# All low parts of the sample's output weights on VectorE, and small buffers given out by how long they have been free

## The chip, the cores and the metric

The kernel runs on one core of a Trainium2 chip. The metric is the device time of one execution in microseconds (us). Before the change it was 1543.17 us, the median of three runs (1542.73, 1543.17 and 1548.15).

## The reference

The kernel computes one layer of an encoder for two inputs that share all weights: a *prompt* of 512 tokens and a *sample* of 1024 tokens, each with 1024 features. Cut to what matters:

```python
h = _rmsnorm(x, norm_attn_g);  z = h @ w_in          # 1024 -> q 512, k 128, v 128, ca 512, cb 512
a_out = _window_attn(q, k, v, bias, band, sink)      # 8 heads, 2 kv heads, |q - k| <= 128
c = _dwconv(ca * sigmoid(cb), conv_dw_w, conv_dw_b)  # 31 taps
c = silu(_layernorm(c, conv_ln_g, conv_ln_b))
x = x + concat([a_out, c]) @ w_out
h = _rmsnorm(x, norm_ffn_g)
u = _dwconv(h @ w_up, ffn_dw_w, ffn_dw_b)            # 3 taps, 2 x 2816 columns
x = x + (silu(u[:, :2816]) * u[:, 2816:]) @ w_down
y = _rmsnorm(x, norm_final_g)
```

Everything is float32. To keep its precision on TensorE, each operand is split into a high part (rounded to the engine's reduced format) and a low part (the rest), and each product is three matmuls: high x high, low x high, high x low.

## The kernel before

**Stages.** The program is written as a main stream of TensorE work with a *side* generator that feeds other work between its pieces. In order:

1. The prompt's `w_in` projection.
2. The sample's `w_in` projection: 14 chunks of 128 columns of `w_in` by two halves of 512 tokens. Its side is `prompt()`: the attention of the prompt (units 0 to 7), the normalisation of its conv branch (`conv_norm`), and the prompt's `w_out` product (`out_half`). The 31 taps of the convolutions are offered to VectorE, ScalarE and GpSimd all the while.
3. The prompt's up projection with its gate (`ffn_step`, 22 steps). Its side is `sample()`: the attention of the sample (units 8 to 23), and then loads and splits of the sample's `w_out` and half of its conv normalisation.
4. The sample's `w_out` product, its up and down projections (with sums and differences of halves that save products; TensorE's order there is written out by hand), and the final norms.

**Who sets the order.** A list scheduler decides, when the program is built, in which order each engine gets its instructions, up to stage 4's hand-written part; it follows the dependences among instructions, and the buffers are among them. Each engine then takes its instructions strictly in that order, so an instruction that waits holds up all that stand behind it on that engine. Another buffer for a tile means another dependence, and so another order on every engine.

**Buffers.** `Slots` hands out SBUF buffers by size: 2 KB buffers (names `h...`), 4 KB ones (`q...`, 15 of them) and two more kinds (`c`, `d`). A request of at most 2 KB (one 128x512 float32 tile) takes the first free buffer of the smallest size that fits; only when none under 4 KB is free is a `q` buffer cut into two halves, as long as more than `KEEP` = 3 of them are free. "First" means the one that has stood longest in the list of free buffers; but a tile can be "free" in this sense while transfers or instructions on it are still to run, and the next owner waits for them.

**Weights.** A chunk is loaded from HBM as raw float32, then `split` makes the high part (`L202`, a cast on ScalarE) and the low part (`L203`, a subtraction raw - high, on GpSimd, or on VectorE if `dve` is set). For `w_in` and `w_up` a chunk is 128x1024 and all low parts are on GpSimd. For the sample's `w_out` there are 16 chunks of 128x512, split in `sample()` by

```python
split_wo((m - WOA) // 2, m % 2, m % 4 < DW2)     # DW2 = 0: none on VectorE
```

**Names and lines.** Products of `w_in` and `w_up` are `L309`, `L310` and `L312` (tiles `b` and `u` in PSUM, two banks each). `b` is emptied by ScalarE `L385`, `L398` and VectorE `L394`, `L399`, `L409`; the rows of q go to HBM by `L403` (`qsd`). Attention: scores `L585`, `L592`, `L603` to `L620`; transposes `L641`, splits `L643`, `L644`, values `L655`, `L656`; rows to HBM `L671` (`catd`). Taps: `L353`, `L356` on ScalarE, `L357` on GpSimd, `L364`, `L372` on VectorE. `conv_norm`: transposes of the conv rows `L700` (PE), statistics `L702`, `L703` (VectorE), reciprocal root `L186`, `L187` (GpSimd), scaling `L706` (VectorE), transposes back `L712` (PE), swish `L715` to `L720`. `w_out`: loads `L761`, `L763`, products `L736` to `L738`. Up projection's gate: `u` is read by ScalarE `L866` and twice by VectorE `L862`; `L886`, `L888`, `L889`, `L891`, `L892` make the gate, `L893` stores it.

Of the kernel before, what the change touches and what calls it, by code (L numbers as in the profile page):

```python
# [15 lines left out]
P = 128  # L16
# [31 lines left out]
SCB, SCD = "aapa", "aaap"  # L48


WOP, WOA, DW, DW2 = 1, 5, 2, 0
NE = 2
YN = 2
OB = "uc"
# [4 lines left out]

BACK = (200, 1500)  # L60
U0 = 2


FILL = 216
# [2 lines left out]
class Slots:  # L67
# [3 lines left out]


    def __init__(self, pool, classes, halved=None, keep=0):
        self.pool, self.free, self.n = pool, [], 0
        self.halved, self.keep, self.halves = halved, keep, {F32: [], F32R: []}
        for kind, (count, size) in classes.items():
            for i in range(count):
                self.free.append((f"{kind}{i}", size))

    def tile(self, shape, dt=F32, nbytes=4, among=None):  # L80
        need = nbytes
        for s in shape:
            need *= s
        fits = [s for s in self.free if s[1] >= need and (among is None or s[0][0] in among)]
        if self.halved and nbytes == 4 and need <= 2048 and not any(s[1] < 4096 for s in fits):
            halves = self.halves[dt]
            if not halves and sum(s[0][0] == self.halved for s in fits) > self.keep:
                slot = next(s for s in fits if s[0][0] == self.halved)
                self.free.remove(slot)
                self.n += 1  # L90
                whole = Whole(self, slot, dt, (self.pool(slot[0]) if callable(self.pool) else self.pool).tile([P, 2, 512], dt, tag=slot[0], name=f"{slot[0]}_{self.n}", bufs=1))
                halves += [(whole, 0), (whole, 1)]
                whole = None
            if halves:
                return Half(*halves.pop(0), shape)
        if not fits:
            raise RuntimeError(f"no slot for {need} bytes")
        least = min(s[1] for s in fits)
        slot = next(s for s in fits if s[1] == least)
        self.free.remove(slot)  # L100
        self.n += 1
        return Held(self, slot, (self.pool(slot[0]) if callable(self.pool) else self.pool).tile([P] + list(shape), dt, tag=slot[0], name=f"{slot[0]}_{self.n}", bufs=1))


class Held:
# [4 lines left out]
        return self.t[i]  # L110

    def __del__(self):
        self.slots.free.append(self.slot)


class Whole:
# [6 lines left out]
class Half:  # L123
# [14 lines left out]
    def __del__(self):  # L138
        w = self.whole
        w.out -= 1  # L140
        if w.out:
            w.slots.halves[w.dt].append((w, self.i))
        else:
            w.slots.halves[w.dt] = [h for h in w.slots.halves[w.dt] if h[0] is not w]
            w.slots.free.append(w.slot)


@with_exitstack
def tile_hybrid_encoder(ctx: ExitStack, tc: tile.TileContext, xs, rel_bias, norm_attn_g, w_in,
# [17 lines left out]
    sb = Slots(lambda tag: homes[tag[0]], dict(q=(15, 4096), c=(4, 4224), h=(61, 2048), d=(2, 2176), s=(32, 64)), "q", KEEP)  # L167
# [133 lines left out]
    def drain(queue):  # L301
        while queue:
            advance(queue)
# [422 lines left out]
    def out_half(i, n):  # L726
        G, b = blocks[i]
        if i not in xr:
            xr[i] = load_x(G, b)
        x = xr[i]  # L730
        po = bank("out")
        s = slice(n * NT, (n + 1) * NT)
        for kc in range(KC):
            wh, wl = wo[kc, n]
            ch, cl = (t[:, kc % 4, :] for t in cats[i, kc // 4])
            nc.tensor.matmul(po[:], ch, wh[:], start=(kc == 0), stop=False)  # L736
            nc.tensor.matmul(po[:], ch, wl[:], start=False, stop=False)  # L737
            nc.tensor.matmul(po[:], cl, wh[:], start=False, stop=(kc == KC - 1))  # L738
            if kc % 2 == 1 and kc < KC - 1:
                yield 0.0  # L740
        nc.vector.tensor_tensor(x[:, s], po[:], x[:, s], op=ALU.add)
        if n == 1:
            x1[i] = x
            nc.sync.dma_start(x1d[i][:], x[:])
            ss = sm(1)
            junk = sb.tile([D], BF16, 2)
            nc.scalar.activation(junk[:], x[:], AF.Square, accum_out=ss[:])
            rstd_of(ss[:], D, rs2[:, i:i + 1])
            cats.pop((i, 0)), cats.pop((i, 1))
            xr.pop(i)  # L750
        yield 0.0
# [83 lines left out]
    drain(side)  # L835
    load_kv()
    drain(convs)


    def want_up(k, half):  # L840
# [103 lines left out]
    for k in range(NJ):  # L944
        if k == U0:
            side.append(sample())
# [418 lines left out]
    need = {1: B11, 2: B21, 5: B12, 6: B22, 4: B21, 3: B22}  # L1365
# [305 lines left out]
```

## Time and profile before

| | us |
|---|---|
| median of three runs | 1543.17 |
| the profiled execution, its own time | 1547.91 |
| its span in the profile | 1546.1 |
| TensorE busy | 1491.7 (96%) |
| VectorE busy | 1125.0 (73%) |
| ScalarE busy | 795.3 (51%) |
| GpSimd busy | 704.0 (46%) |

The profiled execution is 4.7 us over the median of the runs shown. TensorE has 54.4 us in which no matmul runs. Stage 2 lies at about 109 to 318 us of the span, stage 3 at about 350 to 670, the sample's `w_out` product behind it to about 790. In the profile, "PE" is TensorE, "DVE" VectorE, "ACT" ScalarE, "POOL" GpSimd, "SP" the queue that issues the transfers; the column PEclk is the mean clock granted to TensorE, 1.00 being full speed.

### The profile page before, as it was taken

The page shows a single profiled execution, that of the slowest core. Times are in us where ns is not written, and L with a number is a line of the kernel's source. Part 1 is how long each engine was busy: PE and PEld are TensorE (multiplying, and loading weights), DVE is VectorE, ACT ScalarE, POOL GpSimd, SP SyncE. Part 2 cuts the span into 40 slices and gives each one's busy share as a digit, 9 for nine tenths or more (in the row PEclk, how much of TensorE's full clock was granted, in tenths as well). Part 3 has the DMA queues.
Part 4 walks back from the last instruction along what each step waited for, and adds up shares of the span by engine and source line. Part 5 has one row for each costly group of instructions (what it writes and reads, how often), then busy time and mean ns, then how long its engine had stood idle before and what let it go on. Part 6 is the DMA issues. An engine that isn't in the chain of part 4 may idle for free.

```text
span 1546.1 us, 20081 instructions
## 1 busy us (share of the span) xinstructions
PE 1491.7 (96%) x6843; PEld 1228.5 (79%) x6843; DVE 1125.0 (73%) x1608; ACT 795.3 (51%) x1404; POOL 704.0 (46%) x562
## 2 busy tenths in 40 slices
PE   8999998899999999899999999999999899999998
PEld 6787787787888888777777888888888788888886
DVE  7998767857879795434677777777776855668885
ACT  4644654335777776713454544555445633343355
POOL 7652343225667766956423555555545000003345
PEclk9999999899999999999999999999999999999999
DMA  6572334447344435868422233333331582356654
GB/s 226 163 216 80 104 102 125 130 132 223 103 130 130 131 121 165 257 215 287 158 82 69 96 107 105 102 103 102 103 133 51 194 299 86 108 166 214 211 184 163
DMA packets 228780, 227.17 MB, mean 147 GB/s; under 512 B 13268, under 2 KB 168348, under 8 KB 228549
## 3 DMA queue, kind: packets, MB, share of 16 engines
q1 hardware_dynamic: 228677, 225.88, 45.4%
q8 instruction: 54, 0.88, 0.2%
q14 instruction: 49, 0.40, 0.1%
HBM read 164.74 MB, written 62.14 MB: 147 GB/s over the span
## 4 chain that ended last, share of the span: by engine, by line
PE 72%; DMA 4%; DVE 2%; POOL 2%; ACT 2%; issue 1%; SPq 1%; POOLq 0%; ACTq 0%; DVEq 0%
PE w L1091 8%; PE w L1090 8%; PE w L1089 8%; PE w L1423 7%; PE w L1424 7%; PE w L1425 7%; PE u L312 5%; PE u L309 5%; PE u L310 5%; PE u L736 1%; PE u L738 1%; PE u L737 1%; DMA h<-gt 1%; PE b L309 1%; PE b L310 1%
## 5 line engine op out<-in xcount | busy, mean ns | idle before, releaser
L203 POOL TENSOR_TENSOR q<-q,q 128x1024 fp32r<-128x1024 f32 x72 | 173.5, 2415 | 93.6 <-ACT q L202 37.6
L965 POOL TENSOR_TENSOR q<-q,q 128x512 fp32r<-128x512 f32 x101 | 140.7, 1399 | 157.9 <-ACT q L1075 145.8
L965 DVE TENSOR_TENSOR h<-h,h 128x512 fp32r<-128x512 f32 (+2 forms) x202 | 158.2, 816 | 63.1 <-ACT h L969 24.3
L1423 PE MATMUL w<-h,h 128*128 128x512 f32 x462 | 179.8, 389 | 0.6 <-ACT h L969 0.6
L1425 PE MATMUL w<-h,h 128*128 128x512 f32 x462 | 179.8, 389 | 0.0
L1424 PE MATMUL w<-h,h 128*128 128x512 f32 x462 | 179.7, 389 | 0.0
L1089 PE MATMUL w<-h,q 128*128 128x512 f32 x448 | 175.1, 391 | 3.9 <-ACT w L1181 2.2
L1091 PE MATMUL w<-h,q 128*128 128x512 f32 x448 | 174.5, 389 | 1.1 <-POOL q L965 1.1
L309 PE MATMUL u<-h,q 128*128 128x512 f32 x400 | 160.0, 400 | 7.7 <-DVE h L862 4.6
L1090 PE MATMUL w<-h,q 128*128 128x512 f32 x426 | 165.8, 389 | 0.0
L310 PE MATMUL u<-h,q 128*128 128x512 f32 x400 | 157.9, 395 | 0.0
L312 PE MATMUL u<-h,q 128*128 128x512 f32 x384 | 152.4, 397 | 1.3 <-POOL q L203 1.3
L364 DVE SCALAR_TENSOR_TENSOR c<-c,cvw,c 128x512 f32<-128x512 f32 x184 | 138.0, 750 | 2.9
L962 POOL TENSOR_TENSOR q<-q,q 128x1024 f32<-128x1024 f32 x12 | 32.8, 2742 | 235.6 <-DMA h<-gb 195.5
L969 ACT CAST h<-h 128x512 fp32r<-128x512 f32 x120 | 71.7, 620 | 96.7 <-DVE h L965 47.7
L309 PE MATMUL b<-h,q 128*128 128x512 f32 x256 | 102.8, 401 | 4.0 <-DVE d L394 2.9
L1089 PEld LDWEIGHTS w<-h,q 128*128 128x128 f32 x448 | 84.1, 188 | 22.5 <-ACT w L1181 2.6
L862 DVE SCALAR_TENSOR_TENSOR h<-u,fw,h 128x511 f32<-128x511 f32 x88 | 65.4, 743 | 50.3 <-ACT h L866 49.5
L1423 PEld LDWEIGHTS w<-h,h 128*128 128x128 f32 x462 | 86.7, 188 | 19.1 <-ACT h L969 1.0
L310 PE MATMUL b<-h,q 128*128 128x512 f32 x256 | 101.5, 396 | 0.0
L312 PE MATMUL b<-h,q 128*128 128x512 f32 x256 | 101.5, 396 | 0.0
L1425 PEld LDWEIGHTS w<-h,h 128*128 128x128 f32 x462 | 86.7, 188 | 18.1
(417 smaller groups left out, 3656.1 us busy)
## 6 DMA issues: line engine op xcount, KB each, us to landing
q<-in_w_up SPq DMA_DIRECT2D x88, 512.0 KB
ga<-q SPq DMA_DIRECT2D x64, 256.0 KB
h<-ga SPq DMA_DIRECT2D x57, 256.0 KB
q<-in_w_in SPq DMA_DIRECT2D x28, 512.0 KB
h<-in_w_down SPq DMA_DIRECT2D x52, 256.0 KB
q<-in_x_sample SPq DMA_DIRECT2D x15, 512.0 KB
h<-qsd SPq DMA_DIRECT2D x24, 256.0 KB
x1d<-q SPq DMA_DIRECT2D x11, 512.0 KB
```

Source lines behind the costliest of these rows:

```text
L203: (nc.vector if dve else nc.gpsimd).tensor_tensor(lo[:], raw[:], hi[:].bitcast(F32), op=ALU.subtract)
L309: nc.tensor.matmul(out, whi[:, kc, :], hi[:], start=(kc == 0), stop=False)
L310: nc.tensor.matmul(out, whi[:, kc, :], lo[:], start=False, stop=False)
L312: nc.tensor.matmul(out, wlo[:, kc, :], hi[:], start=False, stop=(kc == KC - 1))
L364: nc.vector.scalar_tensor_tensor(acc[:], src(t), w(t), acc[:], op0=ALU.mult, op1=ALU.add)
L965: (eng or nc.vector).tensor_tensor(out, a, b, op=ALU.subtract)
L1089: nc.tensor.matmul(out, whi[:, s], hi[:], start=(start and c == 0), stop=False, **go)
L1090: nc.tensor.matmul(out, whi[:, s], lo[:], start=False, stop=False, **go)
L1091: nc.tensor.matmul(out, wlo[:, s], hi[:], start=False, stop=(stop and c == 3), **go)
L1423: nc.tensor.matmul(out, sh[:, c], th[:], start=(p == 0), stop=False)
L1424: nc.tensor.matmul(out, sh[:, c], tl[:], start=False, stop=False)
L1425: nc.tensor.matmul(out, sl[:, c], th[:], start=False, stop=(p == NPAIR - 1))
```

## The change

Two parts.

1. `DW2` goes from 0 to 4: the low parts of all 16 chunks of the sample's `w_out` are made on VectorE.
2. `Slots` counts its requests (`clock`) and notes at which count each buffer or half buffer came free. A request of at most 2 KB now takes the one of (first free small buffer, oldest free half) that has been free longer. While `sb.old` is 24 (stage 2 from the point at which its side is added, until its rest is drained; 0 elsewhere), a `q` buffer may also be cut in two when the small buffer came free fewer than 24 requests ago and the first free `q` buffer has been free for longer than it; 3 free `q` buffers are still kept whole.

```diff
-WOP, WOA, DW, DW2 = 1, 5, 2, 0
+WOP, WOA, DW, DW2 = 1, 5, 2, 4
...
+OLD = 24
...
+    def give(self, slot):
+        self.since[slot[0]] = self.clock
+        self.free.append(slot)
+
+    def split_whole(self, slot, dt):
...
+        since = self.since.get(slot[0], -OLD)
+        self.halves[dt] += [(whole, 0, since), (whole, 1, since)]
+
     def tile(self, shape, dt=F32, nbytes=4, among=None):
+        self.clock += 1
...
-        if self.halved and nbytes == 4 and need <= 2048 and not any(s[1] < 4096 for s in fits):
+        least = min((s[1] for s in fits), default=0)
+        slot = next((s for s in fits if s[1] == least), None)
+        if self.halved and nbytes == 4 and need <= 2048:
             halves = self.halves[dt]
...
+            wholes = [s for s in fits if s[0][0] == self.halved]
+            since = self.since.get(slot[0], -OLD) if slot and slot[1] < 4096 else self.clock
+            if halves and (min(h[2] for h in halves) < since or since == self.clock):
+                return Half(*self.oldest(halves), shape)
+            if (since == self.clock or self.clock - since < self.old) and len(wholes) > self.keep and \
+                    self.since.get(wholes[0][0], -OLD) < since:
+                self.split_whole(wholes[0], dt)
+                return Half(*self.oldest(halves), shape)
...
     side.append(prompt())
+    sb.old = OLD
...
     drain(convs)
+    sb.old = 0
```

What the change does to the instructions shows at three places. In the listings each row is a line of code, an operation, its output and inputs and its shape; numbers behind a name count buffers and tiles. In the changed kernel the lines of the code have moved by 20 (`L309` to `L329`, `L700` to `L720`, `L712` to `L732`, `L202` to `L222`, `L203` to `L223`) or 22 (`L862` to `L884`, `L866` to `L888`).

The first place is TensorE at the end of the conv normalisation of the prompt, near the end of stage 2. Before:

```order
L310 MATMUL b_149_2657<-h_106_666,q_382_2515 128x512
L312 MATMUL b_149_2657<-h_105_665,q_383_2516 128x512
L700 MATMUL a_142_2526<-ident,q_370_2402 128x128 x4
L712 MATMUL u_144_2556<-ident,q_387_2538 128x128 x4
L700 MATMUL a_150_2684<-ident,h_400_2676 128x128 x4
L712 MATMUL u_152_2717<-ident,h_404_2696 128x128 x4
L655 MATMUL a_148_2618<-h_391_2600,h_162_970 128x512
L736 MATMUL u_154_2828<-h_418_2781,h_216_1325 128x512
```

And now, at the last of the four conv blocks:

```order
L330 MATMUL b_151_2694<-h_150_884,q_364_2497 128x512
L720 MATMUL a_150_2669<-ident,h_385_2661 128x128 x4
L332 MATMUL b_151_2694<-h_149_883,q_365_2498 128x512
L329 MATMUL b_153_2791<-h_83_541,q_380_2637 128x512
L330 MATMUL b_153_2791<-h_84_542,q_380_2637 128x512
L332 MATMUL b_153_2791<-h_83_541,q_381_2638 128x512
L329 MATMUL b_153_2791<-h_85_557,q_380_2637 128x512
L330 MATMUL b_153_2791<-h_86_558,q_380_2637 128x512
L332 MATMUL b_153_2791<-h_85_557,q_381_2638 128x512
L756 MATMUL u_154_2809<-q_247_1580,q_205_1264 128x512
```

Before, the two transposes there and the two back of the last two blocks stood one behind the other with no projection between. Now 34 matmuls of 128x512 (projection and `w_out`) stand between the last block's transposes and its transposes back, and many more between those of the block before; and some tiles of 2 KB are named `q` now (`q_247`, `q_205`).

The second place is ScalarE near the end of stage 3, where it empties the products `u` and casts the high parts of `w_out`. Before:

```order
L866 ACTIVATE h_1003_6447<-u_362_6380,vecs,fw 128x512
L202 CAST h_1052_6643<-h_1031_6549 128x512
L202 CAST h_1035_6563<-h_1014_6490 128x512
L886 ACTIVATE b_364_6522<-h_1003_6447 128x512
L202 CAST h_1012_6480<-h_990_6399 128x512
L866 ACTIVATE h_1022_6512<-u_363_6455,vecs,fw 128x512
L202 CAST h_1015_6492<-h_997_6428 128x512
```

And now:

```order
L222 CAST h_1022_6572<-h_1008_6517 128x512
L888 ACTIVATE h_983_6427<-u_362_6360,vecs,fw 128x512
L908 ACTIVATE b_364_6502<-h_983_6427 128x512
L888 ACTIVATE h_1002_6492<-u_363_6435,vecs,fw 128x512
L222 CAST h_995_6472<-h_977_6408 128x512
L222 CAST h_1015_6543<-h_994_6470 128x512
L222 CAST h_1024_6588<-h_999_6486 128x512
```

The three casts that stood between the emptying of `u_362` and that of `u_363` are gone from there.

The third place is VectorE in the same stretch. Before:

```order
L862 SCALAR_TENSOR_TENSOR h_980_6362<-u_358_6315,fw,h_980_6362 128x511 x2
L665 TENSOR_TENSOR h_979_6349<-b_360_6331,h_957_6218 64x512
L862 SCALAR_TENSOR_TENSOR h_1003_6447<-u_362_6380,fw,h_1003_6447 128x511 x2
L888 SCALAR_TENSOR_TENSOR b_364_6522<-b_364_6522,h_1003_6447 128x512
L862 SCALAR_TENSOR_TENSOR h_1022_6512<-u_363_6455,fw,h_1022_6512 128x511 x2
```

And now:

```order
L884 SCALAR_TENSOR_TENSOR h_960_6342<-u_358_6295,fw,h_960_6342 128x511 x2
L223 TENSOR_TENSOR h_1010_6520<-h_986_6442,h_1009_6519 128x512
L223 TENSOR_TENSOR h_979_6412<-h_969_6376,h_978_6411 128x512
L223 TENSOR_TENSOR h_1018_6554<-h_991_6458,h_1017_6553 128x512
L223 TENSOR_TENSOR h_988_6445<-h_971_6382,h_987_6444 128x512
L223 TENSOR_TENSOR h_1033_6624<-h_1011_6529,h_1032_6623 128x512
L685 TENSOR_TENSOR h_959_6329<-b_360_6311,h_937_6198 64x512
L223 TENSOR_TENSOR h_1023_6573<-h_1008_6517,h_1022_6572 128x512
L884 SCALAR_TENSOR_TENSOR h_983_6427<-u_362_6360,fw,h_983_6427 128x511 x2
L910 SCALAR_TENSOR_TENSOR b_364_6502<-b_364_6502,h_983_6427 128x512
L884 SCALAR_TENSOR_TENSOR h_1002_6492<-u_363_6435,fw,h_1002_6492 128x511 x2
```

Six of the 16 subtractions now stand on VectorE between the reads of `u_358` and those of `u_362`; the others stand in small groups before and behind.

More of the change, by code (lines that the diff above doesn't have):

```diff
@@ L73, in __init__ @@
     def __init__(self, pool, classes, halved=None, keep=0):
-        self.pool, self.free, self.n = pool, [], 0
+        self.pool, self.free, self.n, self.clock, self.since, self.old = pool, [], 0, 0, {}, 0
         self.halved, self.keep, self.halves = halved, keep, {F32: [], F32R: []}
@@ L78, in __init__ @@
                 self.free.append((f"{kind}{i}", size))
+    def give(self, slot):
+        self.since[slot[0]] = self.clock
+        self.free.append(slot)
+    def split_whole(self, slot, dt):
+        self.free.remove(slot)
+        self.n += 1
+        t = (self.pool(slot[0]) if callable(self.pool) else self.pool).tile([P, 2, 512], dt, tag=slot[0], name=f"{slot[0]}_{self.n}", bufs=1)
+        whole = Whole(self, slot, dt, t)
+        since = self.since.get(slot[0], -OLD)
+        self.halves[dt] += [(whole, 0, since), (whole, 1, since)]
     def tile(self, shape, dt=F32, nbytes=4, among=None):
+        self.clock += 1
         need = nbytes
@@ L84, in tile @@
         fits = [s for s in self.free if s[1] >= need and (among is None or s[0][0] in among)]
-        if self.halved and nbytes == 4 and need <= 2048 and not any(s[1] < 4096 for s in fits):
+        least = min((s[1] for s in fits), default=0)
+        slot = next((s for s in fits if s[1] == least), None)
+        if self.halved and nbytes == 4 and need <= 2048:
             halves = self.halves[dt]
[L87 to L96, printed above, removed]
+            wholes = [s for s in fits if s[0][0] == self.halved]
[6 more added lines that the diff above has]
+                return Half(*self.oldest(halves), shape)
+        if slot is None:
             raise RuntimeError(f"no slot for {need} bytes")
-        least = min(s[1] for s in fits)
-        slot = next(s for s in fits if s[1] == least)
         self.free.remove(slot)
@@ L102, in tile, with oldest @@
         return Held(self, slot, (self.pool(slot[0]) if callable(self.pool) else self.pool).tile([P] + list(shape), dt, tag=slot[0], name=f"{slot[0]}_{self.n}", bufs=1))
+    @staticmethod
+    def oldest(halves):
+        h = min(halves, key=lambda h: h[2])
+        halves.remove(h)
+        return h[0], h[1]
 class Held:
@@ L112, in __del__ @@
     def __del__(self):
-        self.slots.free.append(self.slot)
+        self.slots.give(self.slot)
 class Whole:
@@ L141, in __del__ @@
         if w.out:
-            w.slots.halves[w.dt].append((w, self.i))
+            w.slots.halves[w.dt].append((w, self.i, w.slots.clock))
         else:
-            w.slots.halves[w.dt] = [h for h in w.slots.halves[w.dt] if h[0] is not w]
-            w.slots.free.append(w.slot)
+            w.slots.halves[w.dt][:] = [h for h in w.slots.halves[w.dt] if h[0] is not w]
+            w.slots.give(w.slot)
 @with_exitstack
```

## The prediction

> **What bounds the kernel now.** I read the page first: who is busy, and the chain that ended last.
>
> ```profile
> PE 1491.7 (96%) x6843; PEld 1228.5 (79%) x6843; DVE 1125.0 (73%) x1608; ACT 795.3 (51%) x1404; POOL 704.0 (46%) x562
> PE 72%; DMA 4%; DVE 2%; POOL 2%; ACT 2%; issue 1%; SPq 1%; POOLq 0%; ACTq 0%; DVEq 0%
> ```
>
> TensorE is the bound. Neither part of the change removes a matmul, so it can only win PE's idle time and the time in which PE runs at a lower clock. The windows, by stage (us, then busy time of PE, PEld, DVE, ACT, POOL, then PEclk), say where these lie:
>
> ```profile
> 109.00:171.00 62.00, 56.00 (x265) 45.35 (x263) 57.24 (x121) 32.36 (x80) 16.25 (x11) 0.97 0.34 101
> 171.00:260.00 89.00, 87.71 (x422) 72.44 (x423) 64.34 (x123) 49.85 (x107) 38.08 (x28) 1.00 0.43 121
> 260.00:285.00 25.00, 16.80 (x69) 13.22 (x68) 13.29 (x22) 11.62 (x22) 10.21 (x10) 0.80 0.45 142
> 390.00:610.00 220.00, 220.00 (x1070) 185.06 (x1069) 179.17 (x353) 168.71 (x325) 147.88 (x92) 1.00 0.41 129
> 610.00:670.00 60.00, 55.35 (x251) 45.23 (x250) 22.85 (x40) 34.99 (x61) 49.95 (x33) 0.97 0.70 222
> 690.00:790.00 100.00, 94.26 (x451) 76.92 (x450) 59.53 (x88) 35.75 (x74) 54.35 (x75) 1.00 0.61 201
> 790.00:1546.00 756.00, 742.66 (x3304) 612.12 (x3302) 549.06 (x609) 361.37 (x585) 271.81 (x203) 1.00 0.41 135
> ```
>
> The change works in stage 2 (109 to 318) and at the end of stage 3 (610 to 690). Between them PE has no gap at all (390 to 610), and the instruction order there is nearly unchanged: nothing to win. The waits of PE that lie in the two places, in total, times and longest:
>
> ```profile
> PE u L309 <- DVE h L862: 4.6, 2, 3.5
> PE u L712 <- DVE q L706: 4.0, 1, 4.0
> PE u L712 <- DVE h L706: 3.4, 1, 3.4
> PE u L736 <- DVE s L703: 2.2, 1, 2.2
> PE u L309 <- ACT h L270: 2.2, 1, 2.2
> PE u L641 <- DVE s L592: 2.0, 2, 1.0
> ```
>
> Each of the long ones is followed by a lower clock (same columns as the windows above):
>
> ```profile
> 270.00:275.00 5.00, 1.50 (x10) 1.30 (x11) 2.93 (x6) 3.23 (x7) 2.48 (x4) 0.65 0.53 167
> 275.00:280.00 5.00, 4.19 (x12) 3.08 (x11) 2.00 (x4) 3.75 (x9) 2.36 (x2) 0.50 0.44 155
> 280.00:285.00 5.00, 5.00 (x20) 4.00 (x19) 5.00 (x9) 2.13 (x4) 0.20 (x1) 0.83 0.89 279
> 367.00:371.00 4.00, 4.00 (x17) 3.23 (x16) 2.40 (x4) 2.06 (x4) 3.84 (x4) 0.57 0.74 234
> 658.00:662.00 4.00, 4.00 (x13) 3.16 (x13) 0.00 (x0) 0.00 (x0) 4.00 (x5) 0.68 0.59 197
> ```
>
> I price the clock as PE's busy time x (1 - clock): 0.5 + 2.1 + 0.85 = 3.5 us at 270 to 285, 1.7 us at 367, 1.3 us at 658. So a stall of 2.2 us or more costs itself and some 1.5 us behind it.
>
> The Trainium skill ("TensorE: Matmul & The Clock Gate", "What's actually happening") says that the clock halves after an idle window of about 3.4 us. Here 2.2 us of idle at 363 to 365 was enough; by the page that stall would cost 2.2 us and no clock, and the term for it below would be smaller by 1.7 us at most.
>
> **The change, part by part.**
>
> *Term 1: the stall at 266 to 282.* The timeline:
>
> ```profile
> 268.40 0.19 POOL L186 TENSOR_SCALAR s<-s 128x1 f32<-128x1 f32 x1
> 269.28 0.81 DVE L706 TENSOR_SCALAR q<-a,s,s 128x512 f32<-128x512 f32 x1 [2.21 <-POOL s L187]
> 270.14 0.66 PE L712 MATMUL u<-ident,q 128*128 128x128 f32 x4 [4.03 <-DVE q L706]
> 274.60 1.09 PE L712 MATMUL u<-ident,h 128*128 128x128 f32 x4 [3.36 <-DVE h L706]
> 276.92 0.79 PE L736 MATMUL u<-h,h 128*128 128x512 f32 x1 [0.81 <-ACT h L202]
> 280.92 0.63 PE L309 MATMUL b<-h,q 128*128 128x512 f32 x1
> ```
>
> PE transposes a conv block (`L700`) and must then wait for statistics, GpSimd's root and VectorE's scaling before it may transpose back (`L712`); nothing else stands between, twice in a row. Idle 4.03 + 3.36 + 0.81 = 8.2 us, clock 3.5 us: 11.7 us. In the new order at least 34 matmuls stand between. At one per 0.227 us (17 of them start from 261.65 to 265.28) that is 7.7 us,
>
> ```profile
> 261.65 0.39 PE L310 MATMUL b<-h,q 128*128 128x512 f32 x1
> 265.28 0.39 PE L312 MATMUL b<-h,q 128*128 128x512 f32 x1
> ```
>
> which covers the chain of 4.0 us. What the new order adds there: `w_out` products stand in the middle of the projection, and their weights, whose loads share the queue of SP with those of `w_in`, may be late; and tiles in halves of `q` buffers make a chunk of `w_in` wait. Bounds 0 (the stall comes back whole at another place) to -11.7. I give 3.5 us back, the size of one of the two stalls: **-8.2**.
>
> *Term 2: the stall of 2.2 us at 363.* In the new order one cast stands ahead of six taps instead of behind them, so that the first `L270` may come about 1 us sooner. Bounds 0 to -(2.2 + 1.7) = -3.9. I take **-1.5**: a shorter stall, with the clock drop less likely.
>
> *Term 3: the end of stage 3.* GpSimd is the busiest helper at 610 to 670 (50.0 of 60 us). The change takes 20.2 us off it and puts 16 subtractions on VectorE, which idles 37 of these 60 us. What each costs there:
>
> ```profile
> L203 POOL TENSOR_TENSOR h<-h,h 128x512 fp32r<-128x512 f32 x16 | 20.2, 1293 | 0.0
> L203 DVE TENSOR_TENSOR h<-h,h x12: 675/691/693, 222.3 to 319.9; 128x512 fp32r<-128x512 f32 x12
> 289.50 2.65 POOL L203 TENSOR_TENSOR q<-q,q 128x1024 fp32r<-128x1024 f32 x1 [0.17 <-ACT q L202]
> 291.26 1.45 DVE L203 TENSOR_TENSOR q<-h,h 128x512 fp32r<-128x512 f32 x1
> ```
>
> 0.69 us each alone, but the one that began inside a 2.65-us instruction of GpSimd ended 0.55 us after it and took 1.45. So 16 x 0.69 to 16 x 1.45 = 11 to 23 us, which VectorE's 37 idle us hold. But GpSimd's end here frees no one: PE's waits are elsewhere.
>
> ```profile
> 642.88 1.53 DVE L862 SCALAR_TENSOR_TENSOR h<-u,fw,h 128x511 f32<-128x511 f32 x2 [4.79 <-ACT h L866]
> 650.04 0.78 ACT L866 ACTIVATE h<-u,vecs,fw 128x512 f32<-128x512 f32 x1
> 652.54 0.47 PE L309 MATMUL u<-h,q 128*128 128x512 f32 x1 [1.15 <-DVE h L862]
> 652.69 0.62 ACT L202 CAST h<-h 128x512 fp32r<-128x512 f32 x1 [1.36 <-DMA h<-in_w_out]
> 654.26 0.77 ACT L866 ACTIVATE h<-u,vecs,fw 128x512 f32<-128x512 f32 x1
> 656.74 0.47 PE L309 MATMUL u<-h,q 128*128 128x512 f32 x1 [3.50 <-DVE h L862]
> ```
>
> ScalarE sits in front of a cast whose load of `w_out` lands at 652.69, and the emptying of `u_363` stands behind it. In the new order no cast of `w_out` stands there, so 3.5 us and the clock's 1.3 should go. Against that, six subtractions and one `L665` now stand between VectorE's reads of `u_358` (done at 644.41) and of `u_362` (from 650.82): 6.4 us hold 7 x 0.69 = 4.8, but not 6 x 1.45 + 0.69 = 9.4, which would be 3 us late, and PE waits for that one already (1.15). The 2.2 us at `L736` may go too, since `u_368` is now emptied before `u_370` is. Bounds: -(4.8 + 1.15 + 2.2) = -8.2; and, if all six are slow and a stall of 3 us brings its clock drop while nothing else is won, +4. Nearest to the rows with no cast ahead, less a part for the slow subtractions: **-4.0**.
>
> The Trainium skill ("SBUF — State Buffer", "Who interferes with whom") states the mechanism: VectorE with two SBUF inputs and GpSimd reading SBUF lock each other out for a whole instruction. The 1.45 us agrees. By the page the long GpSimd instructions left there (128x1024) would hold VectorE each time; the third rival prices this.
>
> *Term 4: 109 to 171.* VectorE is the bound there (57.2 of 62 us busy), and the change takes nothing off it. The new order puts a longer run of attention matmuls without projection near 150; I add **+2.0**, the two waits on `L592` once more (bounds 0 to +4, with a clock drop).
>
> From 690 on: PE's 5.7 us of idle up to 790 wait for conv rows and norms that no part touches, and from 790 PE is busy 98%. No term.
>
> Sum: -8.2 - 1.5 - 4.0 + 2.0 = -11.7 us. Against the profiled execution's own 1547.9 that is 1536.2; that execution was 4.7 us over the median of the runs, so against the median **1531.5 us**.
>
> **The rivals.** What a measurement of this kernel can tell from no change is about 0.5%, or 7.7 us: faster is below 1535.5, slower above 1550.9.
>
> *The stall moves.* An in-order PE that no longer stops at `L712` stops at the next late thing: `w_out` weights, or the emptying of `b`. For it: VectorE is 92% busy up to 171, and stalls of one kind follow each other there. Against: at 171 to 260 PE has 1.3 us idle in 89. Term 1 is then 0: -3.5 in all, 1539.7 us, no change.
>
> *Weights late: slower.* A `q` buffer in two halves is free only when the last transfer out of both is done; a chunk of `w_in` that takes it waits for the slower. The row exists already:
>
> ```profile
> POOL q L203 <- DMA qsd<-q: 11.0, 1, 11.0
> ```
>
> PE didn't feel it. A chunk serves 48 matmuls, 10.9 us; if its low part (2.4 us) waits 11.0 us each time, it is 2.5 us late, and with a clock drop of 1.7 each costs 4.2. Some four chunks after 170 take such buffers in the new order: +16.8 - 11.7 = +5, **1548 us**; it decides against the change from three late chunks on (+0.9), and beyond 7.7 us from five on (+9.3, 1552.5 us). At 109 stage 2 has 12 chunks left, by the window of `L309` alone (196 matmuls, 16 a chunk):
>
> ```profile
> 109.00:320.00 211.00, 78.10 (x196) 37.29 (x196) 0.97 0.39 116
> ```
>
> *VectorE becomes late at stage 3's end.* GpSimd and VectorE lock each other out there: term 3 at +2 instead of -4.0, so -5.7 in all, 1537.5 us, no change.
>
> **Chances and range.** The forecast 0.57, the stall that moves 0.12, the lockout 0.11, late weights 0.20, of which 0.13 for five chunks or more and 0.07 for three or four. A small part of the forecast's own spread (0.02) lies above 1535.5. Faster 0.55; no change 0.02 + 0.12 + 0.11 + 0.07 = 0.32; slower 0.13. The best bounds of terms 1 to 3 with term 4 as taken give 1543.2 - 23.8 + 2 = 1521.4; at the other end four late chunks give 1548 and five 1552.5. Range 1521 to 1551.
>
> **What would show it.** Term 1: no `L712` (now `L732`) wait over 1 us and PEclk near 1 at 260 to 290. Term 3: no PE wait on `L862` (now `L884`) over 2 us at 640 to 660, and the moved subtractions near 0.7 us rather than 1.5. Term 4: PE's idle at 109 to 171 no more than 8 us. It is wrong if PE waits for `L203` (now `L223`) or `L202` (now `L222`) at 170 to 320 for more than 5 us in all.

## The result and the profile after

The changed kernel takes 1539.38 us (median of 22 runs, 1535.31 to 1545.61), the kernel before 1544.39 us (22 runs, 1539.58 to 1548.48). The ratio is 0.9972, with a 95% interval of 0.9961 to 0.9984: by it the change is 4.3 us faster (2.5 to 6.0). Forecast were 11.7 us less and a time of 1531.5.

The profiled execution of the changed kernel took 1537.94 us, with a span of 1536.1 us. Against the profiled execution of before that is 10.0 us less, so two profiles side by side show almost the forecast. But the one of before lay 3.5 us over the median of its 22 runs and the one of after 1.4 us under its own. So half of the difference between the two profiles is the luck of two executions.

The windows of the changed kernel by stage (us, then busy time of PE, PEld, DVE, ACT, POOL, then PEclk, DMA share, GB/s):

```profile
109.00:171.00 62.00, 56.28 (x276) 45.96 (x275) 57.57 (x123) 36.52 (x89) 15.41 (x10) 1.00 0.39 114
171.00:260.00 89.00, 88.35 (x417) 73.59 (x418) 65.56 (x122) 44.63 (x95) 35.72 (x28) 0.96 0.32 92
260.00:285.00 25.00, 20.86 (x87) 16.18 (x86) 15.43 (x19) 14.97 (x27) 14.74 (x10) 0.93 0.83 245
610.00:670.00 60.00, 54.10 (x241) 43.43 (x241) 44.45 (x52) 31.15 (x53) 28.67 (x16) 0.94 0.66 202
```

At 260 to 285 PE is busy 20.9 us in place of 16.8, with the clock at 0.93 in place of 0.80: the stall at `L712` went. At 171 to 260 the clock was 1.00 before and is 0.96 now: 3.5 us lost that were not lost before. At 610 to 670 VectorE's busy time doubled, from 22.9 to 44.5 us, GpSimd's fell from 50.0 to 28.7, and PE gained nothing: 54.1 us busy against 55.4, at a lower clock.

PE's waits of the changed kernel, in total, times and longest:

```profile
PE u L329 <- DVE h L884: 3.8, 1, 3.8
PE w L1445 <- ACT q L1230: 3.8, 1, 3.8
PE a L605 <- DVE q L664: 1.9, 1, 1.9
PE a L605 <- DVE c L384: 1.9, 1, 1.9
PE a L675 <- ACT h L663: 1.6, 1, 1.6
PE a L732 <- DVE h L726: 0.7, 1, 0.7
```

The two waits of `L712` (now `L732`) of 4.0 and 3.4 us are gone. The wait on the second read of `u` (`L862`, now `L884`) stays at 3.8 us, in one piece where it was 3.5 and 1.15. Attention matmuls (`L605`, `L675`) wait longer at a time: 1.9, 1.9 and 1.6 us, where before the longest such waits were 1.6 and twice 1.0.

To see where each part of the time goes I mark seven points of TensorE's work that every kernel reaches, and take the time between them from the traces: the starts of the 467th and of the 671st matmul of the projections `L309`, `L310`, `L312` (both in stage 2, on either side of its longest rows of attention matmuls), the first transpose of the prompt's second norm (end of stage 2), the 1101st and the 1901st of these matmuls (in stage 3), the last of them, and the first product of the sample's up projection. "Low parts" says how many of the 16 are on VectorE. All in us, one profiled execution each:

| kernel | low parts | to 467th | to 671st | to norm | to 1101st | to 1901st | to last | to up | to end |
|---|---|---|---|---|---|---|---|---|---|
| before | 0 | 156.9 | 65.4 | 128.4 | 46.6 | 241.2 | 43.8 | 89.9 | 773.9 |
| 1st run | 16 | 156.9 | 65.5 | 127.1 | 43.2 | 241.2 | 43.5 | 88.0 | 777.8 |
| change | 16 | 154.3 | 69.7 | 121.1 | 41.3 | 241.2 | 46.6 | 85.6 | 776.2 |
| 2nd run | 0 | 153.7 | 69.4 | 122.9 | 42.1 | 241.2 | 43.6 | 90.7 | 775.3 |
| 3rd run | 8 | 155.7 | 69.7 | 120.7 | 41.7 | 241.2 | 43.2 | 84.6 | 775.4 |
| 4th run (change again) | 16 | 158.0 | 69.2 | 120.8 | 41.3 | 241.2 | 46.7 | 87.0 | 776.8 |
| 5th run | 16 | 156.3 | 65.9 | 115.2 | 45.5 | 241.2 | 46.7 | 84.8 | 777.0 |
| 6th run | 16 | 153.7 | 69.2 | 122.2 | 42.2 | 241.2 | 41.5 | 88.0 | 776.6 |
| 7th run | 8 | 157.1 | 65.5 | 116.0 | 45.7 | 241.2 | 43.2 | 86.1 | 775.8 |
| 8th run | 8 | 156.9 | 65.9 | 115.3 | 43.9 | 241.2 | 41.2 | 85.8 | 775.2 |
| 9th run | 0 | 156.4 | 65.5 | 115.8 | 45.1 | 241.2 | 44.2 | 89.6 | 776.0 |
| 10th run | 16 | 160.3 | 65.5 | 115.6 | 46.3 | 241.2 | 44.0 | 87.9 | 778.2 |

A mark must have the same work ahead of it in every order. In all twelve kernels 685 matmuls of all kinds start ahead of the 467th, 991 ahead of the 671st and 1519 ahead of the norm. The 501st, near the 500th that some expectations name, is no such mark: 769 lie ahead of it in the order of the change and 757 in that of before, so some of the difference at it is only work that changed sides. Of the marks from "last" on, small differences remain (up to 8 matmuls at "last", 4 at "up"); the sum from the 1901st to the end is free of them.

The stretch to the 1901st, where nothing stalls, repeats to 0.1 us, and the one to the 671st to 0.5 us within an order. The others vary by up to 4 us between executions of one order.

### The profile page after: what moved, and what is told of

It is laid out like the page before. It is cut to its first block, busy times and chain, and to the rows that moved or that the text cites. A ratio compares the mean times of both kernels' runs of the same rounds, so it can differ in the third digit from the quotient of the medians.

```text
span 1536.1 us, 20070 instructions
## 1 busy us (share of the span) xinstructions
PE 1492.1 (97%) x6843; PEld 1229.9 (80%) x6843; DVE 1151.4 (75%) x1624; ACT 795.9 (52%) x1404; POOL 693.2 (45%) x546
## 4 chain that ended last, share of the span: by engine, by line
PE 50%; DMA 3%; DVE 2%; POOL 1%; issue 1%; ACT 1%; SPq 1%; POOLq 0%; DVEq 0%; ACTq 0%
PE w L1113 8%; PE w L1111 8%; PE w L1112 8%; PE w L1445 7%; PE w L1447 7%; PE w L1446 7%; DMA q<-in_w_up 1%; DMA h<-in_w_down 1%; DMA h<-gt 1%; PE u L756 1%; PE u L757 1%; PE u L758 1%; PE u L329 1%; PE u L330 1%; PE u L332 1%
## 5 line engine op out<-in xcount | busy, mean ns | idle before, releaser
L223 POOL TENSOR_TENSOR q<-q,q 128x1024 fp32r<-128x1024 f32 x72 | 175.1, 2438 | 115.8 <-ACT q L222 43.7
L987 DVE TENSOR_TENSOR h<-h,h 128x512 fp32r<-128x512 f32 (+2 forms) x202 | 154.1, 795 | 66.1 <-DMA h<-in_w_down 27.6
L1445 PE MATMUL w<-h,h 128*128 128x512 f32 x458 | 179.0, 391 | 3.8 <-ACT q L1230 3.8
L329 PE MATMUL u<-h,q 128*128 128x512 f32 x400 | 161.5, 404 | 4.8 <-DVE h L884 3.8
L329 PE MATMUL b<-h,q 128*128 128x512 f32 x256 | 102.9, 402 | 4.6 <-DVE d L414 2.3
L1445 PEld LDWEIGHTS w<-h,h 128*128 128x128 f32 x458 | 86.3, 189 | 22.0 <-ACT q L1230 4.2
L1447 PEld LDWEIGHTS w<-h,h 128*128 128x128 f32 x462 | 87.0, 188 | 18.1
L1446 PEld LDWEIGHTS w<-h,h 128*128 128x128 f32 x458 | 86.4, 189 | 18.1
L222 ACT CAST q<-q 128x1024 fp32r<-128x1024 f32 (+1 forms) x73 | 76.0, 1045 | 48.0 <-POOL q L223 17.4
```

Source lines behind the costliest of these rows:

```text
L223: (nc.vector if dve else nc.gpsimd).tensor_tensor(lo[:], raw[:], hi[:].bitcast(F32), op=ALU.subtract)
L329: nc.tensor.matmul(out, whi[:, kc, :], hi[:], start=(kc == 0), stop=False)
L987: (eng or nc.vector).tensor_tensor(out, a, b, op=ALU.subtract)
L1445: nc.tensor.matmul(out, sh[:, c], th[:], start=(p == 0), stop=False)
L1446: nc.tensor.matmul(out, sh[:, c], tl[:], start=False, stop=False)
L1447: nc.tensor.matmul(out, sl[:, c], th[:], start=False, stop=(p == NPAIR - 1))
```

## The experiments

**Part 1 alone (1st run).** The kernel before with

```diff
-WOP, WOA, DW, DW2 = 1, 5, 2, 0
+WOP, WOA, DW, DW2 = 1, 5, 2, 4
```

> Part 1 alone: the buffers as before, all 16 low parts of the sample's output weights on VectorE. Instruction order is that of the kernel before up to about 630 us. Theory A (the two parts add, and the two profiled executions are typical): stage 3's end pays for the lockout, so this is 0 to +3 us against before, and its profile has the stalls of 4.0 and 3.4 us at 266 to 282 again, with the 1100th matmul of the projections at 397 us, as in the profile of before. Theory B (the profiled execution of before was a slow one, which is why the profiles differ by 10 us and the medians by 5): the time is the same, but that 1100th matmul comes 3 us or more before 397. Theory C (part 1 is what gained, part 2 nothing): 4 to 5 us faster.

Measured: ratio 1.0031 (1.0016 to 1.0046), 4.8 us slower. Theory C falls: part 1 gained nothing by itself. Theory A's 0 to +3 us are exceeded too, and theory B expected no change in time. Up to about 630 us the order is that of the kernel before, and the stall at `L712` is there again; but the 1101st matmul comes at 392.7 us, not 397.3. Of the 4.6 us, 3.4 lie between the norm and that matmul: there the profile of before had the wait of 2.2 us on `L270` at 363 with a clock drop behind it, and this one has neither (only a wait of 1.5 us on a low part at 371). So this part of theory B is borne out by one more execution, and a part of the 10 us was probably never the change's. But this profiled execution (1545.02 us) is the fastest of the run's twelve, 2.6 us under their median, as that of before is a slow one; and with 1543.2 us its span is shorter than that of before, while the medians say 4.8 us longer. Where the 4.8 us lie is therefore not shown. The one stretch that is longer than before is the last, by 3.9 us.

**Part 2 alone (2nd run).** The changed kernel with `DW2` at 0.

> Part 2 alone: the new choice of buffers, the low parts on GpSimd as before. Order is that of the changed kernel up to about 630 us. Theory A: the stage-2 gain without the lockout, 5 to 8 us faster than before, and faster than the changed kernel by 1 to 3 us; at 640 to 650 no wait of PE on the last read of u (L884) of 3 us unless a cast waits for a load as before. Theory C: no change against before.

Measured: ratio 0.9979 (0.9964 to 0.9994), 3.2 us faster, against 0.9979 (0.9963 to 0.9995) for the changed kernel on the same chip (4th run). With part 2's order in place, part 1 adds nothing: what the change gains is part 2's. (The parts don't add: part 1 alone cost 4.8 us.) The expectation was 5 to 8 us, and it left out what the row of the table shows beside the 5 us won from the 671st matmul to the norm: 4.0 us lost between the 467th and the 671st.

**Half of the low parts (3rd run).** The changed kernel with `DW2` at 2: of each four chunks two on VectorE.

> The changed kernel with 8 of the 16 low parts back on GpSimd (those of every other pair). Order is that of the changed kernel up to the last products of the projection. If VectorE and GpSimd lock each other out per instruction, GpSimd is busier here, so each of the 8 subtractions on VectorE still takes 0.7 to 2.9 us, but there are only half of them: the wait of PE at u_362 is between 0 and 3.8 us; the time between 4 us under before and the time of part 2 alone. If the lockout plays no part, the same as the changed kernel within 1 us.

Measured: ratio 0.9952 (0.9934 to 0.9970), 7.4 us faster than before and, by the medians on one chip, 4 us faster than the changed kernel (the intervals of the two ratios just overlap), against both expectations. The lockout is there: the 8 subtractions take 1.83 us on average. PE still waits 4.3 us for the read of `u_362`, so the stretch to the last projection gains 3.4 us by other means: the waits of 0.8 and 1.2 us for `catd` just ahead of it are gone, and the clock drop behind it is 3.4 us long, not 6.8.

**The change again (4th run).** No edit.

> The changed kernel once more, on the chip of the other three, for the comparison and for a second profile. Theory A: 4 to 5 us faster than before; its profile repeats the times of the first one at the 500th, 1100th and last matmul of the projections within 2 us. Theory B for this kernel: they differ by 3 us or more, at places where the clock was lower in one of the two.

Measured: ratio 0.9979 (0.9963 to 0.9995). Its profile repeats the stretches of the first one within 1.5 us but for the first stretch, which is 3.7 us longer: a wait that begins near 121 us was 4.4 us long instead of 1.9, with a clock drop behind it. And of PE's two kinds of waits ahead of the last projection, `L884` took 2.2 us here and 3.8 there, `catd` 3.5 and 2.0. One profile places a stall well and sizes it badly.

**Cutting for age from a later chunk on (5th run).** In the changed kernel:

```diff
-    sb.old = OLD
+    sb.old = 0
...
-        want_raw(i + 2)
+        sb.old = OLD if i >= npr + 4 else 0; want_raw(i + 2)
```

> The changed kernel, but q buffers may be cut for age only from the 5th of the sample's chunks of w_in on. TensorE's order up to about 170 us is then the one of the kernel before (27 attention matmuls without projection near 150, not 36), while at the end of the stage 31 to 42 matmuls still stand between a conv block's transposes and its transposes back. Theory: the loss at 109 to 178 comes from that order. Then the 500th matmul of the projections comes at 174 to 176 us (178 to 182 in the four profiles with the new order, 174.4 in the two with the old one), the gain of stage 2's end stays, and the time is 2 to 5 us under the changed kernel. Rival: the loss comes from the state of the buffers as such, or the gain is tied to it; then the 500th is at 178 or later, or the stall of 4 and 3 us is back.

Measured: ratio 0.9949 (0.9930 to 0.9968), 7.9 us faster than before. The 501st matmul comes at 174.3 us again; at the marks with equal work, the stretch from the 467th to the 671st takes 65.9 us, as in the kernel before (65.4) and not 69.7. The stretch behind it keeps its gain and adds 5.9 us to it; behind the norm 4.2 of that go again, at a wait of 2.6 us for `L806`. The rival falls: the loss between the 467th and the 671st belongs to the order of that place (69.2 to 69.7 in all five kernels with the one order, 65.4 to 65.9 in all seven with the other), and the gain can be had without it. Of the 7th to the 10th run, with the same edit, three have the 501st matmul at 174.0 to 174.9; the 10th had a wait of 1.7 us near 123 with a clock drop and came to 177.9. The windows of this run, to be read against those above:

```profile
109.00:171.00 62.00, 54.78 (x266) 44.48 (x264) 57.60 (x122) 33.46 (x81) 16.58 (x11) 1.00 0.34 101
171.00:178.00 7.00, 6.92 (x33) 5.83 (x34) 1.78 (x5) 4.14 (x11) 2.52 (x2) 1.00 0.52 150
260.00:285.00 25.00, 24.64 (x113) 20.14 (x112) 17.72 (x21) 14.16 (x25) 11.11 (x9) 1.00 0.81 235
```

In the changed kernel the same place, around its waits of 1.3, 1.9 and 1.0 us between 165 and 172, reads:

```profile
164.00:172.00 8.00, 3.75 (x23) 2.62 (x21) 7.69 (x19) 7.98 (x22) 2.04 (x2) 0.91 0.16 59
172.00:178.00 6.00, 6.00 (x17) 4.75 (x17) 3.32 (x7) 2.17 (x5) 1.72 (x2) 0.55 0.58 175
```

and in the kernel before:

```profile
164.00:172.00 8.00, 5.53 (x32) 4.13 (x31) 7.03 (x18) 7.86 (x22) 2.39 (x3) 1.00 0.13 41
172.00:178.00 6.00, 6.00 (x28) 4.96 (x27) 1.18 (x3) 3.61 (x9) 2.94 (x4) 1.00 0.59 168
```

VectorE and ScalarE are busy 7 to 8 of the 8 us in both. The changed kernel has 42 matmuls, nearly all of the attention, with no projection between them from 160.3 to 174.6 us; the longest such row there before has 30. From 164 to 172 PE idles 4.3 us in place of 2.5, and from 170.6 us on it runs 6.8 us at half clock.

**GpSimd's long instructions cut in two (6th run).** The changed kernel with the low parts of the last three pairs of chunks of `w_up` in halves; the values are the same:

```diff
-        (nc.vector if dve else nc.gpsimd).tensor_tensor(lo[:], raw[:], hi[:].bitcast(F32), op=ALU.subtract)
+        [(nc.vector if dve else nc.gpsimd).tensor_tensor(lo[:, s], raw[:, s], hi[:, s].bitcast(F32), op=ALU.subtract) for s in ([slice(0, KC // 2), slice(KC // 2, KC)] if halves else [slice(None)])]
...
-            upw[k, half] = split(upr.pop((k, half)))
+            upw[k, half] = split(upr.pop((k, half)), halves=k >= 19)
```

> The changed kernel with the low parts of the last three pairs of chunks of w_up made in two GpSimd instructions of 128x512 each in place of one of 128x1024. The order of the instructions stays, but for one subtraction that trades places with a read of u. Theory (each VectorE subtraction that begins inside a GpSimd instruction waits for its end, then takes 0.55 us): the ones between the reads of u_358 and u_362 fall from 2.86 to about 1.85 us each, the read of u_362 comes about 3 us sooner, PE's wait of 3.5 to 3.8 us there falls to 1 us or less, and the time is 3 to 5 us under the changed kernel (the wait and the half clock behind it). Rival (the two engines share bandwidth, or the wait has another cause): the subtractions together take as long as before, and the wait stays at 3 us or more.

Measured: ratio 0.9971 (0.9957 to 0.9986), that of the changed kernel (0.9972), so no gain in time. The mechanism shows all the same. The timeline of the changed kernel, VectorE and then GpSimd:

```profile
633.04 1.52 DVE L884 SCALAR_TENSOR_TENSOR h<-u,fw,h 128x511 f32<-128x511 f32 x2
634.48 10.77 DVE L223 TENSOR_TENSOR h<-h,h 128x512 fp32r<-128x512 f32 x5
645.27 0.69 DVE L685 TENSOR_TENSOR h<-b,h 64x512 f32<-64x512 f32 x1
646.73 1.54 DVE L884 SCALAR_TENSOR_TENSOR h<-u,fw,h 128x511 f32<-128x511 f32 x2
...
636.36 8.34 POOL L223 TENSOR_TENSOR q<-q,q 128x1024 fp32r<-128x1024 f32 x3
```

Five subtractions take 10.8 us, in step with GpSimd's three long ones: the trace has them one by one as 0.68, 1.79, 2.89, 2.86 and 2.86 us. And in the 6th run:

```profile
635.60 5.79 DVE L223 TENSOR_TENSOR h<-h,h 128x512 fp32r<-128x512 f32 x4
641.41 0.69 DVE L685 TENSOR_TENSOR h<-b,h 64x512 f32<-64x512 f32 x1
643.10 1.53 DVE L884 SCALAR_TENSOR_TENSOR h<-u,fw,h 128x511 f32<-128x511 f32 x2
...
637.39 9.29 POOL L223 TENSOR_TENSOR q<-q,q 128x512 fp32r<-128x512 f32 x6
```

Now each takes 0.68 to 1.78 us, GpSimd 9.3 us in place of 8.3, and the read of `u_362` starts at 643.1 rather than 646.7. All 16 subtractions take 18.1 us in place of 23.0; the rival had their total stay. PE's wait fell only to 2.8 us, not to 1 (the unhalved order itself had 3.8 and 2.2 in its two profiles), but PE's idle time from the 1901st matmul to the last is 3.2 us in place of 5.9 and 5.8. And there was no clock drop, where the changed kernel had 6.8 us at half clock:

```profile
645.00:652.00 7.00, 3.59 (x9) 2.87 (x10) 6.11 (x10) 1.80 (x3) 1.71 (x1) 0.51 0.54 155
```

The stretch from the 1901st matmul to the last is 5.2 us shorter than in the changed kernel (41.5, against 46.6 and 46.7), and from the 1901st to the end this profile is still 2.3 and 4.4 us shorter than the two of the changed kernel. But this execution took 1536.26 us, 4.0 less than the median of its twelve. So what takes the gain back in most executions isn't shown. A candidate lies behind: at 779 PE waits 3.2 us for the last norm of the sample's rows, with 3.4 us of half clock.

```profile
781.87 0.33 PE L1034 MATMUL t<-ident,q 128*128 128x128 f32 x1 [3.22 <-DVE q L1009]
783.00:787.00 4.00, 4.00 (x20) 3.60 (x18) 3.97 (x8) 1.76 (x3) 0.00 (x0) 0.57 0.01 2
```

This wait is not in the changed kernel. The order of the last `w_out` products is another here, the same as in the 1st and the 10th run, and these three are the ones that have a wait of 3.2 us there. None of the three was faster than the kernel that it was to improve on; no run changes that order alone.

**Later start and half of the low parts (7th run).** The 5th run's edit and `DW2` at 2.

> The later start of the 5th run with 8 of the 16 low parts on VectorE as in the 3rd. If the parts add: the 3rd run's time (1535.7) less what the 5th gains over the changed kernel, so 1531 to 1534.

Measured: ratio 0.9914 (0.9894 to 0.9934), 1531.91 us, as expected: the gains of the 3rd and of the 5th run add.

**All three (8th run).** The 7th with the 6th's halves.

> As the 7th, with the last low parts of w_up in halves as in the 6th. In the 3rd run PE still waited 4.3 us at u_362 for subtractions of 1.4 to 2.9 us; with the halves these are at most 1.85 us, so that wait falls to 1.5 us or less and the time to 1527 to 1532. If the lockout isn't what holds VectorE up, the same as the 7th.

Measured: ratio 0.9895 (0.9874 to 0.9915), 1528.31 us, 16 us under the kernel before and 11 under the changed one; it has the lowest median here (its interval overlaps with the 7th's). PE's wait for `u_362` is 2.2 us (4.3 in the 7th run's order), more than the 1.5 expected:

```profile
PE u L329 <- DVE h L884: 2.2, 1, 2.2
```

Here the order of the last `w_out` products has no wait of 3.2 us, and the 2.0 us that the halves gain up to the last projection stay.

**Later start and no low part on VectorE (9th run).** The 5th run's edit and `DW2` at 0.

> The later start of the 5th run with none of the 16 low parts on VectorE (part 1 undone; the 7th run has 8 of them there, the 5th all 16). Theory (all 16 on VectorE buy nothing, since they trade GpSimd's time for the lockout; 8 buy some): within 2 us of the 5th run (1535.5), 2 to 5 us over the 7th (1531.9). Rival (part 1 is a gain by itself that stage 2 hid): 4 us or more over the 5th.

Measured: ratio 0.9941 (0.9926 to 0.9956), 1535.21 us: within 1.2 us of the 5th run (0.9949). So with this order of stage 2 all 16 on VectorE are worth nothing, and 8 are worth about 4 us (0.9914 against 0.9941, intervals that just overlap; with the changed kernel's order the 3rd run lies 3.9 us under the 2nd on one chip). Why 8 gain what 16 don't isn't shown beyond the price of the lockout.

**Later start, all 16, halves (10th run).**

> The 5th run (all 16 low parts on VectorE) with the last low parts of w_up in halves, as in the 6th. If the lockout is the price of part 1, the subtractions between the reads of u_358 and u_362 take 1.8 us rather than 2.85, PE's wait of 2.3 us for the read of u_362 and the 3.2 us behind it at 638 to 645 shrink by 2 us or more together, and the time is 2 to 4 us under the 5th run (1535.5).

Measured: ratio 0.9961 (0.9947 to 0.9976), 1537.15 us, not faster than the 5th run (0.9949): the expected 2 to 4 us did not come. The subtractions took 1.8 us as expected and the stretch to the last projection is 2.7 us shorter, but the order behind it is again the one with the wait of 3.2 us and the clock drop. (This profile is the slowest of the run's six.)

## Why the prediction was wrong

The sum was -11.7 us; the measured gain is 4.3 (2.5 to 6.0). By its steps, sized at the marks with equal work:

- **Term 1, the stall at `L712`: the mechanism right, 2 us too large.** Forecast -8.2. From the 671st matmul to the norm the two profiles of the old order have 128.4 and 127.1 us, the five with the new one (change, 2nd, 3rd, 4th, 6th) 120.7 to 122.9, mean 121.5: -6.2. The 3.5 us given back were meant for late `w_out` weights and for halves of `q` buffers. What came is another: PE stops for the emptying of `b` (`L419`, `L399` before) and for a split of the attention (`L663`), as the first rival had named in part:

```profile
261.57 0.50 PE L329 MATMUL b<-h,q 128*128 128x512 f32 x1 [0.94 <-DVE h L419]
263.90 0.49 PE L675 MATMUL a<-h,h 128*128 128x512 f32 x1 [1.60 <-ACT h L663]
266.74 0.79 PE L329 MATMUL b<-h,q 128*128 128x512 f32 x1 [1.37 <-DVE q L419]
```

  In the 5th run's order these go as well.
- **Term 2, the stall at 363: right in size, by luck.** Forecast -1.5. Against the 1st run (43.2 us to the 1101st) the new order's 41.3 to 42.2 is -1.5; against the profile of before it is -4.9. The 2.2 us and the clock drop that the prediction quoted are not in the 1st run's profile, which has the same order. The prediction took less than half of their price because it expected a shorter stall to be left; in the new order PE idles 0 to 0.8 us in all there. In the first pair of profiles this alone makes 3.4 of the 10 us.
- **Term 4, 109 to 171: right in size, in part by luck.** Forecast +2.0 with a bound of +4. The 671st matmul came at 222.3 and 222.4 us in the old order and at 222.9 to 227.3 in the new, mean 224.5: +2.2. But this is a loss of 4.0 us between the 467th and the 671st less 1.8 us won ahead of the 467th, a gain that the prediction didn't have and that varies by 4 us between executions. The loss is not one more pair of waits on `L592`: in the changed kernel it is waits of 1.3, 1.9 and 1.0 us in the long row of attention matmuls and 6.8 us at half clock. The prediction's sign for this term, PE's idle time at 109 to 171 under 8 us, read 5.7 and so missed it: the half clock begins at 170.6. The 5th run shows that the loss could have been avoided.
- **Term 3, the end of stage 3: the step that failed.** Forecast -4.0, "nearest to the rows with no cast ahead, less a part for the slow subtractions". The cast did go from in front of `u_363`, and the wait there with it. But the 16 subtractions cost the upper bound, not something near the lower: 23.0 us in all, as 16 x 1.45 said, and three of the six between the reads of `u_358` and `u_362` took 2.9 each, twice what the one quoted row showed. VectorE at 610 to 670 of the changed kernel:

```profile
L223 DVE TENSOR_TENSOR h<-h,h 128x512 fp32r<-128x512 f32 x16 | 23.0, 1463 | 2.6 <-ACT h L222 1.9 <-POOL h L914 0.6
```

  ScalarE had emptied `u_362` at 640.9 and VectorE read it at 646.7, 5.8 us later, behind subtractions:

```profile
640.15 0.78 ACT L888 ACTIVATE h<-u,vecs,fw 128x512 f32<-128x512 f32 x1
648.41 0.77 PE L329 MATMUL u<-h,q 128*128 128x512 f32 x1 [3.84 <-DVE h L884]
```

  PE waited 3.8 us in place of 3.5. In the three profiles with all 16 and the same order of that place (change, 4th, 5th) this wait is 3.8, 2.2 and 3.2, PE idles 5.8 to 5.9 us from the 1901st matmul to the last, and the clock drop is 6.8 us long; with none on VectorE (before, 2nd, 9th) the wait is 3.5 each time, PE idles 4.5 to 4.6, and the drop is 3.4, 3.4 and 6.8 us long. So one stall was traded for another, and both of the prediction's signs for this term failed: a wait over 2 us on `L884`, and subtractions of 1.46 us on average in place of 0.7. From the 1901st matmul to the up projection the kernels with all 16 and no halves (1st, change, 4th, 5th) have a mean of 132.3 us, those with none 133.9: -1.6. Behind that they are longer, 776.2 to 777.8 against 773.9 to 776.0: +1.9. So part 1 is worth about 0 in sum, as the change and the 2nd run, and the 5th and the 9th, say by their times. Only without part 2 (1st run) is it a loss of 4.8.
- **"No term" from 690 on: wrong by 2 us or so in these profiles.** The orders behind stage 3 are not fixed: with 16 low parts on VectorE one order of the `w_out` products (1st, 6th, 10th run) has a wait of 3.2 us at its end. Near 1215 us, where the up products end and the down products begin, PE waits at other instructions than before (at the down product `L1445` 2.7 to 5.0 us in the ten kernels with part 2, at the up product `L1089` 2.2 and 1.9 in the two without), but all waits there together are 4.5 us before and 5.4 now. The profile of before, unlike most, has no clock drop behind them, so a part of the 1.9 may be luck again. What sets these waits wasn't tested.

With the measured sizes the sum is -6.2 - 1.5 + 2.2 - 1.6 + 1.9 = -5.2, inside the measured interval. Of the 6.5 us that are short of the forecast, 4.3 are part 1's (-4.0 forecast, +0.3 found) and 2.0 term 1's. What happened is close to the third rival (the lockout, forecast at 1537.5 us with a chance of 0.11). The first rival named almost the measured time (1539.7), but by another way: it had term 1 at 0, and it was -6.2. The rival of late weights did not occur: of PE's waits for low parts of `w_in` in the changed kernel there is one, 1.2 us, at 62 us.

The working also made a mistake of method: it took the sum against one profiled execution and read the clock's losses there as the kernel's. The excess of that execution over the median, 3.5 us, is as large as what it lost in term 2 and the 1st run's profile, in the same order, did not (3.4 us); that the two are the same is not shown. Nor did its price of some 1.5 us of clock behind each stall of 2.2 us or more hold: the last section has a stall of 2.8 us with none.

## What to carry to other kernels

Before work is moved from GpSimd to VectorE, look whether both then read SBUF at the same time: here a subtraction of 0.69 us with two SBUF inputs that began inside a GpSimd instruction ended about 0.55 us after it, so the length of GpSimd's instructions, not VectorE's idle share, set the price; moving only half won where moving all won nothing, and shorter GpSimd instructions made the subtractions shorter, if not always the kernel. The stall of an engine that takes its instructions in order went when other work was put between the two halves of a dependence; the same reordering is best held back from places that were well before. A stall's size wants more than one profile: place it with one, size it with two or more. And a mark for such a comparison must have the same work ahead of it in both orders.

## What was not expected of the hardware

- **The lockout can last longer than one instruction.** The VectorE subtraction at 629.4 us of the changed kernel began inside a GpSimd instruction of 1.3 us and ended only 0.55 us after the following one of 2.4 us: 3.75 us for 0.69 us of work. The same subtraction took 3.76 and 3.75 us in the 4th and 3rd runs, and 3.89 in the 6th and 10th, where three GpSimd instructions went by. The Trainium skill ("SBUF — State Buffer", "Who interferes with whom") says that the order of issue decides which of the two blocks; here a GpSimd instruction that by the profile began 0.8 us after the subtraction still went ahead of it, and the measurement decides. The Trainium skill also says there that a VectorE instruction with at most one SBUF input, outside some faster modes, does not contend with GpSimd. The trace agrees: VectorE's reads of PSUM with one such input (`L884`) took 0.72 to 0.75 us throughout.

```profile
629.37 3.75 DVE L223 TENSOR_TENSOR h<-h,h 128x512 fp32r<-128x512 f32 x1
628.93 1.29 POOL L687 TENSOR_TENSOR h<-h,h 64x512 fp32r<-64x512 f32 x1 [5.16 <-DMA h<-in_w_out]
630.18 2.38 POOL L223 TENSOR_TENSOR q<-q,q 128x1024 fp32r<-128x1024 f32 x1
```

- **The length of a stall does not tell whether the clock drops.** 2.2 us of idle at 363 cost 3.4 us of half clock in the profile of before; 2.8 us at 642 in the 6th run cost none:

```profile
644.78 0.47 PE L329 MATMUL u<-h,q 128*128 128x512 f32 x1 [2.80 <-DVE h L884]
646.00:652.00 6.00, 6.00 (x30) 4.96 (x29) 4.06 (x7) 1.59 (x4) 1.97 (x2) 1.00 0.57 204
```

  In all twelve profiles the drops last 3.4 us or two or three times that, but for the last one of each, which runs past the end of the work. That fits the window of about 3.4 us, free-running, in the Trainium skill ("TensorE: Matmul & The Clock Gate", "What's actually happening"). The drop behind 2.2 us of idle doesn't fit the full idle window that the Trainium skill asks for there, and the measurement decides.
